# Weight low parts by accumulating DMA in the first mixer, weights prepared 1024 wide, and new beginnings of the stages of a two-layer decoder kernel

## The chip, the cores and the metric

The kernel runs on one core of a Trainium2 chip. The metric is the time of one execution in device microseconds (us). The core has a matmul engine (TensorE, PE in the rows; its weight loads, PEld, overlap the matmuls), VectorE (DVE), ScalarE (ACT), GpSimd (POOL) and SyncE (SP). Each engine works through its own queue of instructions in order. DMA transfers are issued by SP, ACT or POOL and then run beside the engines.

## The reference, cut to what matters

512 tokens of width 1024 pass through two layers in float32. `@` is a matrix product.

```
def even_mixer(h):                        # layer 0
    q, k, v, glu = split(h @ w_in)        # 8 query heads, 2 key/value heads, 64 wide
    a = band_attention(rotary(q), rotary(k), v, window 128, sinks)
    c = glu_a * sigmoid(glu_b)            # 512 channels
    c = causal_depthwise_conv(c, 31 taps) + bias
    return concat(a, silu(layer_norm(c))) @ w_out

def odd_mixer(h):                         # layer 1
    dilated windows (128,1), (512,4), (2048,16) mixed by their softmax sums
    || gMLP: u * (lower-triangular mixing of layer_norm(g) per group)
    concatenated, then @ w_out

def swiglu(h):  return (silu(h @ w_gate) * (h @ w_up)) @ w_down     # 2816 wide

for layer in (0, 1):
    h = h + mixer(rms_norm(h));  h = h + swiglu(rms_norm(h))
y = rms_norm(h)
```

## The kernel before

**Products.** Activations lie transposed, as eight tiles h[0] to h[7] of 128 channels by 512 tokens. Every float32 product is made of three matmuls in the fp32r type: a value is split into a high part (its rounding to fp32r) and a low part (the rest), and high by high, high by low and low by high are summed in one PSUM bank. `acc3` issues the three, at L200 (weight high, activation high), L201 (weight high, activation low) and L202 (weight low, activation high), each 128x128 by 128x512. `norm_tile` splits h[k] after multiplying it with the norm's gain: ACT writes xh (L312), DVE writes xl (L313).

**Weights.** All weights lie in HBM as one stream `ws` of blocks 128x1024, in the order in which they are used. `dma_block` (L161) loads a block into a `raw` buffer from SP's queue. `prep_unit` takes half a block, 512 wide: ACT copies it to the high part (L173) and an engine subtracts that from raw to get the low part (L150). That engine is DVE, but GpSimd in the layer-0 mixer after the first two k steps. Three units are prepared ahead of the one in use, and a unit is 12 matmuls.

**Orders.** The order of PE's instructions is written out by hand; `Seq` places the attention steps, the transposes and the norm between the products by written costs and due times (`C0`, `tick`). The orders of the other engines are set by a scheduler when the kernel is built, from priorities and its own timing of the code. The taps of the convolution have a low priority (`LATER`).

**Start.** The first product goes over k = 0 to 7 into two banks as the tiles of h arrive. The RMS norm's sum of squares is made beside it: DVE and ACT square (L333, L335), GpSimd takes k = 0, 1 and 5, DVE adds the two sums (L340), and four matmuls with a column of ones (L343) give the sum per token. `norm_b` (L355 to L358) makes the row factor R from it, which is applied after the products.

**Layer-0 mixer.** Products of q, k, v and the two convolution inputs, with attention (scores L580 and L581, exponentials L600, transposes L406, values L420) placed between them. The key's low part kl is made by DVE (L688), the query's by L707. `conv_tile` (L470 to L479) makes 31 taps for each of four channel tiles. With `taps=(8, 15, 15, 10)`, that many (the first on ACT alone) go by an ACT product (L473) and a GpSimd add (L474); the rest are multiply-adds of DVE into a PSUM bank (L476, L478).

**FFN.** Two blocks of hidden units (f = 0, 1) go through `acc3`, for gate (pg) and up (pu). The others go in groups by seven products of Strassen's kind (L891 to L894): sums of activations s (S1 and the like) by sums of weights. The operands T1 to T4 of the weights are made in memory: ACT writes rows of h times gain (L799, for the activations), GpSimd issues a DMA that adds one block of `ws` onto another block that lies in a raw buffer (L857), ACT makes the high part (L867), DVE the low part (L150, w2l). `norm_a` and `norm_b` stand behind pg and pu of f = 0, then `act` and `sums` (L826 to L829, L810 to L817) make the activation sums.

Of the kernel before, what the change touches and what calls it, by code (L numbers as in the profile page):

```python
# [10 lines left out]
def _warn_once_fixed(msg, *args, **kwargs):  # L11
# [12 lines left out]
P = 128  # L24
S = 512
# [16 lines left out]
    sq_pool=(0, 1, 5), rope_v=('k', 'q2', 'q3'),  # L42
    taps=(8, 15, 15, 10),

    norm=(6.15, 2.0), q=5.99, v=0.5, S=3.13, ST=0.86, TA=0.65, AO=1.09, LB=4.85, LO=2.1, ln=(54.8, 69.91, 96.75, 112.86),
# [43 lines left out]
def order_ffn_in():  # L89
    o = [(w, k, f) for f in GROUPS[0] for w in range(2) for k in range(KT)]  # L90
    return o + [(w, 4 * kh + j, f) for fs in GROUPS[1:] for w, kh in BLOCKS for j in range(4) for f in fs]
# [42 lines left out]
def trunk_kernel(ctx: ExitStack, tc: tile.TileContext, xT, ws, cols, sinks, sgu_g, sgu_b,  # L134
# [18 lines left out]
    RAW_AHEAD, PREP_AHEAD = 3, 3  # L153
# [11 lines left out]
    def prep_unit():  # L165
        u = st["prep"]
        b, half = divmod(u, 2)
        while st["dma"] <= b:
            dma_block()
        src = raws[b][:, half * 512:half * 512 + 512]  # L170
        hi = wpool.tile([P, 512], F32R, name="w_hi", bufs=PREP_AHEAD + 1)
        lo = wpool.tile([P, 512], F32R, name="w_lo", bufs=PREP_AHEAD + 1)
        A.activation(hi, src, AF.Copy)  # L173
        sub(lo_engine[0], lo, src, hi)
        units[u] = (hi, lo)
        st["prep"] += 1
        if half:
            del raws[b]
            if st["dma"] < len(STREAM) and st["dma"] <= b + RAW_AHEAD:
                dma_block()  # L180

    def next_unit():
        u = st["tile"] // 4
        while st["prep"] < min(2 * len(STREAM), u + PREP_AHEAD + 1):
            prep_unit()
        return units[u]

    def next_tile():
        t = st["tile"]
        hi, lo = next_unit()  # L190
        st["tile"] += 1
        j = t % 4
        if j == 3:
            del units[t // 4]
        return hi[:, j * P:(j + 1) * P], lo[:, j * P:(j + 1) * P]
# [48 lines left out]
    def next_row():  # L244
        hi, lo = next_unit()
        st["tile"] += 4
        del units[st["tile"] // 4 - 1]
        return hi, lo
# [35 lines left out]
    st["dma"] = 1  # L284
    nc.sync.dma_start(raw[:, :512], ws[0, :, :512])
    nc.sync.dma_start(cc, cols)
    nc.sync.dma_start(h[0], xT[0])
    nc.sync.dma_start(raw[:, 512:], ws[0, :, 512:])
    for k in range(1, KT):
        nc.sync.dma_start(h[k], xT[k])  # L290
        if k in (2, 4):
            dma_block()
# [5 lines left out]
    V.memset(mhalf, -0.5)  # L298

# [17 lines left out]
    def norm_sq(k, eng=None):  # L317
        if eng is G:
            first = "accg" not in norm
            if first:  # L320
                norm["accg"] = mpool[0].tile([P, S], F32, name="pts", bufs=3)
                G.tensor_mul(norm["accg"], h[k], h[k])
            else:
                sq = mpool[0].tile([P, S], F32, name="prod", bufs=3)
                G.tensor_mul(sq, h[k], h[k])
                G.tensor_add(norm["accg"], norm["accg"], sq)
            return
# [9 lines left out]
    def norm_a(b):  # L337
        acc = norm.pop("acc")
        if "accg" in norm:
            V.tensor_add(acc, acc, norm.pop("accg"))  # L340
        ms = bank(b)
        for t in range(NQ):
            T.matmul(ms[:, t:t + 1], acc[:, t * P:(t + 1) * P], ones, start=True, stop=True)  # L343
        mse = scr.tile([P, 4], F32, name="mse")
# [98 lines left out]
    with ExitStack() as mx:  # L443
# [15 lines left out]

        yc = [mp.tile([P, S], F32, name=f"yc{j}") for j in range(4)]  # L460
# [40 lines left out]
        def sq_eng(k):  # L501
            return G if k in C0["sq_pool"] else None

# [3 lines left out]
        def norm_line():  # L507
            yield 0.0, C0["norm"][0]
            norm_a(6)
            yield 0.75, C0["norm"][1]  # L510
# [9 lines left out]

        for k in range(KT):
            if k < 3:
                norm_tile(k, "ev_g", sq_eng(k))
            if k == 2:
                for q in range(3, KT):
                    norm_tile(q, "ev_g", sq_eng(q))
                seq.add("N", norm_line())
            for n in C0["first"].split():
                acc3(first[n], xs[k], k == 0, k == KT - 1)
            if k == 1:  # L530
                lo_engine[0] = G
# [31 lines left out]
        def scores0(i):  # L563
# [3 lines left out]
            qss = qTs[i][1]  # L567
# [103 lines left out]
        for step in C0["steps"].split():  # L671
# [24 lines left out]
            elif kind == "q":  # L696
                ps = gemm_in(step)
                seq.until(lambda: len(qTs) < 2)
                qTs[i] = (mp.tile([P, S], F32, name="qT", bufs=3),
                          [mp.tile([P, S], F32R, name=f"qs{b}", bufs=2) for b in range(2)])  # L700

                def after(i=i, ps=ps, step=step):
                    qT, qss = qTs[i]
# [18 lines left out]
            elif kind == "Y":  # L722
# [4 lines left out]
                early[i] = mp.tile([P, S], F32, name="qT", bufs=3)  # L727
# [39 lines left out]
    def ffn(layer, gnext):  # L767
        with ExitStack() as fx:
# [9 lines left out]
            def temps():  # L778
                return {"p1": [scr.tile([P, S], F32, name="ga") for _ in range(2)],
                        "p5": [scr.tile([P, S], F32, name="gb") for _ in range(2)],  # L780
                        "u2": [fp.tile([P, S], F32, name="ta", bufs=2) for _ in range(2)],
                        "g2": [fp.tile([P, S], F32, name="tb", bufs=2) for _ in range(2)]}
# [139 lines left out]

            hidden(0)
            for f in GROUPS[0]:
                pg, pu = bank(2 * f), bank(2 * f + 1)
                for k in range(KT):
                    acc3(pg, xs[k], k == 0, k == KT - 1)
                if f == 0:
                    norm_a(6)
                for k in range(KT):  # L930
                    acc3(pu, xs[k], k == 0, k == KT - 1)
                if f == 0:
                    norm_b(7)
                act(f, pg, pu)
                sums(f)
                if f == 0:
                    prep_ops(2)
# [381 lines left out]
```

## Time and profile before

| | us |
|---|---|
| time before, median of 3 | 1125.21 (1124.75 to 1131.72) |
| the profiled execution's own time | 1123.48 |
| its span, first to last instruction | 1121.8 |
| PE busy | 1073.6 (96%) |
| DVE busy | 701.2 (63%) |
| ACT busy | 571.7 (51%) |
| POOL busy | 244.7 (22%) |

The span is what the trace shows, and the profiled execution lasted 1.68 us longer than its span. The median stands 1.73 us above the profiled execution. The mean granted clock of TensorE was 0.979 of full speed. A busy share counts an engine as busy at either clock; it is an average over stages with different limits.

### The profile page before, as it was taken

The numbers are of one execution on the slowest core, as the hardware profiler recorded it, in microseconds if no ns is written. First come the engines' busy times: TensorE is split into PE (matmuls) and PEld (weight loads), VectorE is DVE, ScalarE is ACT, GpSimd is POOL, SyncE is SP. The second block draws the span as 40 slices with busy tenths as digits, with TensorE's granted clock in tenths as the row PEclk, the third lists the DMA queues.
The fourth block names the chain that finished last, engine by engine and source line by source line (L and its number), as shares of the span: only waits on it lengthen the run. The fifth ranks groups of instructions, "written<-read, shape, count | busy, mean of one in ns | idle before, by whom it ended". The sixth has DMA issues, their size and how long they took to land.

```text
span 1121.8 us, 13570 instructions
## 1 busy us (share of the span) xinstructions
PE 1073.6 (96%) x5052; PEld 888.4 (79%) x5052; DVE 701.2 (63%) x1060; ACT 571.7 (51%) x926; POOL 244.7 (22%) x218
## 2 busy tenths in 40 slices
PE   6988999899999999999999999999899999999997
PEld 4867778788888888888887888887688888888785
DVE  6899866677565655664748647655765556555543
ACT  5577756654434353543637654455544443535433
POOL 4898754201101010100024200002111010101002
PEclk9988899899999999999999999999999999999999
DMA  5221112977857676711532111247778577767121
GB/s 216 81 71 57 38 38 92 246 210 190 182 170 162 184 150 199 145 43 57 164 99 75 39 55 59 79 154 184 216 189 180 165 167 182 154 189 150 25 69 75
DMA packets 42802, 145.87 MB, mean 130 GB/s; under 512 B 4848, under 2 KB 5744, under 8 KB 42736
## 3 DMA queue, kind: packets, MB, share of 16 engines
q1 hardware_dynamic: 31216, 103.06, 27.1%
q0 software_dynamic: 11520, 41.95, 22.2%
q8 instruction: 39, 0.64, 0.2%
q14 instruction: 27, 0.22, 0.1%
HBM read 142.89 MB, written 2.10 MB: 129 GB/s over the span
## 4 chain that ended last, share of the span: by engine, by line
PE 77%; DVE 8%; ACT 4%; issue 4%; POOL 4%; DMA 2%; POOLq 0%; SPq 0%; ACTq 0%; DVEq 0%
PE bank L894 11%; PE bank L891 11%; PE bank L893 11%; PE bank L200 10%; PE bank L201 10%; PE bank L202 10%; PE bank L261 2%; PE bank L263 2%; PE bank L262 2%; PE bank L420 2%; POOL yc L474 1%; DMA raw<-in_ws 1%; PE bank L906 1%; PE bank L406 1%; DVE w2l L150 1%
## 5 line engine op out<-in xcount | busy, mean ns | idle before, releaser
L150 DVE TENSOR_TENSOR w2l<-raw,w2h 128x1024 fp32r<-128x1024 f32 x140 | 171.5, 1226 | 200.6 <-ACT w2h L867 199.8
L867 ACT ACTIVATE w2h<-raw 128x1024 fp32r<-128x1024 f32 x140 | 148.0, 1059 | 204.7 <-PE bank L894 161.7
L173 ACT ACTIVATE w_hi<-raw 128x512 fp32r<-128x512 f32 x204 | 128.1, 629 | 185.3 <-PE bank L201 138.8
L857 POOL DMA_DIRECT2D raw<-in_ws x80 | 70.0, 887 | 558.7 <-DMA raw<-in_ws 270.0
L150 DVE TENSOR_TENSOR w_lo<-raw,w_hi 128x512 fp32r<-128x512 f32 x161 | 115.0, 715 | 61.5 <-ACT w_hi L173 61.5
L891 PE MATMUL bank<-w2h,s 128*128 128x512 f32 x320 | 126.2, 394 | 1.7 <-ACT ga L957 1.5
L893 PE MATMUL bank<-w2l,s 128*128 128x512 f32 x320 | 125.3, 391 | 1.8 <-DVE w2l L150 1.8
L894 PE MATMUL bank<-w2h,s 128*128 128x512 f32 x320 | 125.3, 392 | 0.1
L200 PE MATMUL bank<-xh,w_hi 128*128 128x512 f32 x272 | 113.6, 418 | 10.8 <-ACT xh L312 10.8
L201 PE MATMUL bank<-xl,w_hi 128*128 128x512 f32 x272 | 110.8, 407 | 1.9 <-DVE xl L313 1.9
L202 PE MATMUL bank<-xh,w_lo 128*128 128x512 f32 x272 | 110.2, 405 | 0.0
L200 PE MATMUL bank<-hh,w_hi 128*128 128x512 f32 x256 | 99.8, 390 | 0.0
L202 PE MATMUL bank<-hh,w_lo 128*128 128x512 f32 x256 | 99.6, 389 | 0.0
L201 PE MATMUL bank<-hl,w_hi 128*128 128x512 f32 x256 | 99.6, 389 | 0.0
L891 PE MATMUL bank<-w2h,xh 128*128 128x512 f32 x240 | 94.4, 393 | 0.0
L894 PE MATMUL bank<-w2h,xl 128*128 128x512 f32 x240 | 93.5, 390 | 0.0
L893 PE MATMUL bank<-w2l,xh 128*128 128x512 f32 x240 | 93.4, 389 | 0.0
L891 PEld LDWEIGHTS bank<-w2h,s 128*128 128x128 f32 x320 | 60.4, 189 | 14.9 <-ACT ga L957 1.9
L893 PEld LDWEIGHTS bank<-w2l,s 128*128 128x128 f32 x320 | 60.5, 189 | 14.5 <-DVE w2l L150 2.1
L200 PEld LDWEIGHTS bank<-xh,w_hi 128*128 128x128 f32 x272 | 54.1, 199 | 22.4 <-ACT xh L312 11.7
L894 PEld LDWEIGHTS bank<-w2h,s 128*128 128x128 f32 x320 | 60.5, 189 | 13.1 <-DVE s L150 0.4
L150 POOL TENSOR_TENSOR w_lo<-raw,w_hi 128x512 fp32r<-128x512 f32 x43 | 58.9, 1371 | 43.3 <-ACT w_hi L173 37.8
(234 smaller groups left out, 2069.6 us busy)
## 6 DMA issues: line engine op xcount, KB each, us to landing
raw<-in_ws SPq DMA_DIRECT2D x181, 512.0 KB, 4.0
raw<-in_ws POOLq DMA_DIRECT2D x80, 512.0 KB, 5.4
h<-in_xT SPq DMA_DIRECT2D x8, 256.0 KB, 6.5
out_y<-xh SPq DMA_DIRECT2D x4, 256.0 KB, 2.0
out_y<-xl SPq DMA_DIRECT2D x4, 256.0 KB, 2.3
raw<-in_ws SPq DMA_DIRECT2D x2, 256.0 KB, 4.0
ropeC<-in_rope_c SPq DMA_DIRECT2D x2, 256.0 KB, 4.0
ropeS<-in_rope_s SPq DMA_DIRECT2D x2, 256.0 KB, 4.8
```

Of the source, the lines that this page charges most:

```text
L150: eng.tensor_tensor(out=out, in0=a, in1=b, op=ALU.subtract)
L173: A.activation(hi, src, AF.Copy)
L200: T.matmul(ps, hi, xh, start=start, stop=False)
L201: T.matmul(ps, hi, xl, start=False, stop=False)
L202: T.matmul(ps, lo, xh, start=False, stop=stop)
L261: T.matmul(ps[t], xh[:, c], hi, start=(k == 0), stop=False)
L262: T.matmul(ps[t], xh[:, c], lo, start=False, stop=False)
L857: nc.gpsimd.dma_start(t, ws[base + 8 * (g - 1) + 2 * BLOCK_OF[more] + q], accum_op=ALU.add)
L867: A.activation(hi, src, AF.Copy)
L891: T.matmul(ps[t], xh[:, c], wh[:, w], start=(start and j == 0), stop=False, skip_group_check=True)
L893: T.matmul(ps[t], xh[:, c], wl[:, w], start=False, stop=False, skip_group_check=True)
L894: T.matmul(ps[t], xl[:, c], wh[:, w], start=False, stop=(j == 3), skip_group_check=True)
```

## The change

- **Preparation 1024 wide.** `prep_unit` takes a whole block; two blocks are prepared ahead of the one in use, with two raw buffers and three buffers each of high and low parts. Block 0 is still prepared in halves.
- **Low parts by accumulating DMA.** In the layer-0 mixer, once the first loop over k is over, ACT makes a second copy with scale -1 of the high part (L178 of the new kernel), and GpSimd issues a DMA (L179) that adds the block of `ws` onto it in memory. This is so for 20 blocks. Elsewhere the low part is DVE's subtraction.
- **Taps.** `taps=(12, 18, 18, 14)`: 14 more taps go by ACT product and GpSimd add, 58 of DVE's 72 L478 stay.
- **Start.** Five float32 matmuls of 128x256 on zeros stand ahead of the first product. Loads: cc from ACT's queue, h[0] first on SP's. The squares are all made by ACT, and summed by PE, four matmuls with ones for each k (`sq_sum`), between the products.
- **FFN beginnings.** Of f = 0, gate and up take k = 0 to 6 first and k = 7 last. `norm_a` follows f = 0, and `norm_b` with f = 0's activation and sums stands in the middle of f = 1. The operands of T1 are begun ahead of f = 0. One temporary (g2) is dropped.
- Some tiles are placed in other memory: qT in gb, `early` in prod, Pm and qs earlier, uT0 in the place of mask1.

The diff, cut to what the prediction speaks of:

```diff
...
-    sq_pool=(0, 1, 5), rope_v=('k', 'q2', 'q3'),
-    taps=(8, 15, 15, 10),
+    rope_v=('k', 'q2', 'q3'),
+    taps=(12, 18, 18, 14),
...
     def prep_unit():
...
+        b = st["prep"]
         while st["dma"] <= b:
             dma_block()
...
+        hi = wpool.tile([P, 1024], F32R, name="w_hi", bufs=PREP_AHEAD + 1)
+        lo = wpool.tile([P, 1024], F32R, name="w_lo", bufs=PREP_AHEAD + 1)
+        for c in ((slice(0, 512), slice(512, 1024)) if b == 0 else (slice(0, 1024),)):
+            A.activation(hi[:, c], raw[:, c], AF.Copy)
+            if lo_engine[0] is G:
+                A.activation(lo, hi, AF.Copy, scale=-1.0)
+                nc.gpsimd.dma_start(lo, ws[STREAM[b]], accum_op=ALU.add)
+            else:
+                sub(V, lo[:, c], raw[:, c], hi[:, c])
...
+    idle = scr.tile([P, 256], F32, name="sq", bufs=1)
+    V.memset(idle, 0.0)
+    ps = bank(7)
+    for _ in range(5):
+        T.matmul(ps[:, :256], idle[:, :P], idle, start=True, stop=True)
...
+        def sq_sum(k):
+
+            sq = mp.tile([P, S], F32, name="prod", bufs=3)
+            A.activation(sq, h[k], AF.Square)
+            for t in range(NQ):
+                T.matmul(ms[:, t:t + 1], sq[:, t * P:(t + 1) * P], ones, start=(k == 0 and t == 0),
+                         stop=(k == KT - 1), skip_group_check=True)
...
+            prep_ops(2)
+            for q in range(2):
+                source(1, "T1", q)
             hidden(0)
             for f in GROUPS[0]:
...
+                if f == 0:
+
+                    o = [(w, k) for w in range(2) for k in range(KT - 1)] + [(w, KT - 1) for w in range(2)]
+                else:
+                    o = [(w, k) for w in range(2) for k in range(KT)]
+                for i, (w, k) in enumerate(o):
+                    acc3(ps[w], xs[k], k == 0, k == KT - 1)
+                    if f == 1 and i == KT - 1:
+                        norm_b(7)
+                        act(0, *first)
+                        sums(0)
                 if f == 0:
                     norm_a(6)
...
+            act(1, *ps)
+            sums(1)
...
```

On GpSimd's queue in the layer-0 mixer, where the first taps (of the tile yc_125, in the new kernel yc_134) begin, the kernel before has

```order
L474 TENSOR_TENSOR yc_125<-yc_125,prod 128x512 x2
L150 TENSOR_TENSOR w_lo<-raw,w_hi 128x512
L474 TENSOR_TENSOR yc_125<-yc_125,prod 128x512
L150 TENSOR_TENSOR w_lo<-raw,w_hi 128x512
L391 TENSOR_TENSOR rb<-rb,ropeS 128x512
L474 TENSOR_TENSOR yc_125<-yc_125,prod 128x512
L150 TENSOR_TENSOR w_lo<-raw,w_hi 128x512
L392 TENSOR_TENSOR qT<-ra,rb 128x512
```

and the new kernel

```order
L179 DMA w_lo<-in_ws 128x1024 x2
L483 TENSOR_TENSOR yc_134<-yc_134,prod 128x512 x3
L396 TENSOR_TENSOR rb<-rb,ropeS 128x512
L483 TENSOR_TENSOR yc_134<-yc_134,prod 128x512
L179 DMA w_lo<-in_ws 128x1024
L397 TENSOR_TENSOR gb<-ra,rb 128x512
L483 TENSOR_TENSOR yc_134<-yc_134,prod 128x512
L179 DMA w_lo<-in_ws 128x1024
L483 TENSOR_TENSOR yc_134<-yc_134,prod 128x512 x4
```

The subtractions are gone, and one DMA for 1024 columns stands for two of them; each still waits behind the adds (L483) ahead of it.

On ACT's queue at the same place the kernel before has one copy of a half block at a time between the tap products (L473):

```order
L470 ACTIVATE yc_125<-cp_116,cc 128x512
L473 ACTIVATE prod<-cp_116,cc 128x512 x3
L556 ACTIVATE Vt<-bank_410 128x512
L173 ACTIVATE w_hi<-raw 128x512
L473 ACTIVATE prod<-cp_116,cc 128x512
```

and the new kernel has two instructions of twice the width for a block (tap products are L482):

```order
L479 ACTIVATE yc_134<-cp_122,cc 128x512
L482 ACTIVATE prod<-cp_122,cc 128x512 x4
L176 ACTIVATE w_hi<-raw 128x1024
L482 ACTIVATE prod<-cp_122,cc 128x512
L178 ACTIVATE w_lo<-w_hi 128x1024
L482 ACTIVATE prod<-cp_122,cc 128x512 x2
L176 ACTIVATE w_hi<-raw 128x1024
```

The negated copy (L178) is new, and a tap product can stand between it and the high part.

On PE where FFN 0 begins, the kernel before takes the last tile of h (xh_1869) at the end of the gate's product into bank_1882, ahead of all of the up product:

```order
L202 MATMUL bank_1882<-xh_1844,w_lo 128x512
L200 MATMUL bank_1882<-xh_1869,w_hi 128x512
L201 MATMUL bank_1882<-xl_1870,w_hi 128x512
L202 MATMUL bank_1882<-xh_1869,w_lo 128x512
L343 MATMUL bank_1918<-ones,nacc 128x1 x4
L200 MATMUL bank_1883<-xh_1727,w_hi 128x512
```

The new kernel takes it (xh_1859) for gate and up (bank_1888, bank_1889) once both have had the other seven:

```order
L208 MATMUL bank_1889<-xh_1838,w_lo 128x512
L206 MATMUL bank_1888<-xh_1859,w_hi 128x512
L207 MATMUL bank_1888<-xl_1860,w_hi 128x512
L208 MATMUL bank_1888<-xh_1859,w_lo 128x512
L206 MATMUL bank_1889<-xh_1859,w_hi 128x512
L207 MATMUL bank_1889<-xl_1860,w_hi 128x512
L208 MATMUL bank_1889<-xh_1859,w_lo 128x512
L345 MATMUL bank_1950<-ones,nacc 128x1 x4
L206 MATMUL bank_1959<-xh_1727,w_hi 128x512
```

The last tile of h is wanted 21 matmuls later than before, the sum of squares (L345) 24 later.

## Rows read from the trace of the kernel before

**Rows 1.** Windows by stretch: length; busy us (x instructions) per engine; granted clock; DMA share; GB/s.

```profile
26.40:62.40 36.00, 36.00 (x166) 29.88 (x165) 30.95 (x42) 19.39 (x32) 30.49 (x23) 1.00 0.24 74
62.40:106.00 43.60, 35.57 (x188) 29.41 (x187) 41.04 (x92) 35.21 (x80) 39.30 (x30) 0.92 0.19 61
106.10:112.40 6.30, 6.30 (x32) 6.21 (x30) 6.20 (x8) 3.23 (x6) 5.52 (x4) 0.50 0.27 85
112.90:153.80 40.90, 36.09 (x200) 30.80 (x200) 35.85 (x81) 27.94 (x68) 25.53 (x20) 0.88 0.08 27
195.70:226.60 30.90, 27.49 (x113) 22.09 (x113) 21.81 (x33) 20.10 (x32) 7.26 (x7) 0.89 0.94 250
```

**Rows 2.** PE's waits: line, releaser, us in all, times, longest.

```profile
PE bank L581 <- DVE kl L688: 3.5, 2, 2.2
PE bank L406 <- ACT yn L634: 3.4, 2, 2.4
```

**Rows 3.** Timeline of PE at the start: begin, us, operation, [idle before].

```profile
7.41 0.80 PE L200 MATMUL bank<-xh,w_hi 128*128 128x512 f32 x1 [7.41 <-ACT xh L312]
13.28 0.63 PE L202 MATMUL bank<-xh,w_lo 128*128 128x512 f32 x1
15.17 0.39 PE L200 MATMUL bank<-xh,w_hi 128*128 128x512 f32 x1
15.40 0.40 PE L201 MATMUL bank<-xl,w_hi 128*128 128x512 f32 x1
19.38 0.50 PE L201 MATMUL bank<-xl,w_hi 128*128 128x512 f32 x1 [1.08 <-DVE xl L313]
24.82 1.05 PE L343 MATMUL bank<-ones,nacc 128*128 128x1 f32 x8 [1.67 <-DVE nacc L340]
25.73 0.48 PE L200 MATMUL bank<-xh,w_hi 128*128 128x512 f32 x1
```

**Rows 4.** Groups by line and shape, 26.4 to 153.8 us: busy us, mean ns, idle before.

```profile
L474 POOL TENSOR_TENSOR yc<-yc,prod 128x512 f32<-128x512 f32 x44 | 60.2, 1369 | 7.9 <-ACT prod L473 6.4
L478 DVE SCALAR_TENSOR_TENSOR bank<-cp,cc,bank 128x512 f32<-128x512 f32 x72 | 54.1, 752 | 1.3
L150 POOL TENSOR_TENSOR w_lo<-raw,w_hi 128x512 fp32r<-128x512 f32 x26 | 36.0, 1387 | 9.2 <-ACT w_hi L173 9.2
L173 ACT ACTIVATE w_hi<-raw 128x512 fp32r<-128x512 f32 x26 | 16.3, 625 | 8.8 <-PE bank L201 8.5
L473 ACT ACTIVATE prod<-cp,cc 128x512 f32<-128x512 f32 x44 | 30.6, 714 | 5.1 <-POOL yc L474 4.9
L707 DVE TENSOR_TENSOR qs<-qT,qs 64x512 fp32r<-64x512 f32 x8 | 9.3, 1156 | 0.5 <-ACT qs L706 0.2
```

**Rows 5.** Page, costliest groups: busy us, mean ns, idle before.

```profile
L867 ACT ACTIVATE w2h<-raw 128x1024 fp32r<-128x1024 f32 x140 | 148.0, 1059 | 204.7 <-PE bank L894 161.7
L857 POOL DMA_DIRECT2D raw<-in_ws x80 | 70.0, 887 | 558.7 <-DMA raw<-in_ws 270.0
```

**Rows 6.** Page, DMA issues: KB each, median us to landing.

```profile
raw<-in_ws POOLq DMA_DIRECT2D x80, 512.0 KB, 5.4
```

**Rows 7.** Timelines of PE, ACT and DVE where FFN 0 begins.

```profile
203.50 0.49 PE L200 MATMUL bank<-xh,w_hi 128*128 128x512 f32 x1 [2.78 <-ACT xh L312]
198.45 4.38 ACT L799 ACTIVATE raw<-h,cc 128x512 f32<-128x512 f32 x7
216.56 0.69 DVE L826 TENSOR_TENSOR ga<-bank,R 128x512 f32<-128x512 f32 x1 [0.39 <-ACT R L358]
226.65 0.39 PE L891 MATMUL bank<-w2h,xh 128*128 128x512 f32 x1
228.66 0.68 DVE L150 TENSOR_TENSOR s<-ga,s 128x512 fp32r<-128x512 f32 x1
```

**Rows 8.** Timelines of ACT and PE where FFN 1 begins.

```profile
775.09 1.06 ACT L867 ACTIVATE w2h<-raw 128x1024 fp32r<-128x1024 f32 x1 [5.92 <-DMA raw<-in_ws]
791.22 0.50 PE L893 MATMUL bank<-w2l,s 128*128 128x512 f32 x1 [1.78 <-DVE w2l L150]
```

More of the change, by code (lines that the diff above doesn't have):

```diff
@@ L315, in norm_tile, with norm_sq @@
         norm_sq(k, sq)
[L317 to L326, printed above, removed]
+    def norm_sq(k, sq=None):
+        if sq is False:
             return
@@ L458, in trunk_kernel @@
         V.tensor_scalar(out=taps, in0=taps, scalar1=0.5, scalar2=None, op0=ALU.mult)
+        mp.tile([P, 8, 2 * P], F32, name="Pm", bufs=2)
+        for b in range(2):
+            mp.tile([P, S], F32R, name=f"qs{b}", bufs=2)
         yc = [mp.tile([P, S], F32, name=f"yc{j}") for j in range(4)]
@@ L698, in trunk_kernel @@
                 seq.until(lambda: len(qTs) < 2)
-                qTs[i] = (mp.tile([P, S], F32, name="qT", bufs=3),
-                          [mp.tile([P, S], F32R, name=f"qs{b}", bufs=2) for b in range(2)])
+                qTs[i] = [mp.tile([P, S], F32R, name=f"qs{b}", bufs=2) for b in range(2)]
                 def after(i=i, ps=ps, step=step):
-                    qT, qss = qTs[i]
+                    qT, qss = scr.tile([P, S], F32, name="gb"), qTs[i]
                     rope(ps, qT, tabs, V if step in C0["rope_v"] else G)
@@ L726, in trunk_kernel @@
                     acc3(ps, (oh[k], ol[k]), k == 0, k == 3)
-                early[i] = mp.tile([P, S], F32, name="qT", bufs=3)
+                early[i] = mp.tile([P, S], F32, name="prod", bufs=3)
                 A.activation(early[i], ps, AF.Copy)
@@ L780, in temps @@
                         "p5": [scr.tile([P, S], F32, name="gb") for _ in range(2)],
-                        "u2": [fp.tile([P, S], F32, name="ta", bufs=2) for _ in range(2)],
-                        "g2": [fp.tile([P, S], F32, name="tb", bufs=2) for _ in range(2)]}
+                        "u2": [fp.tile([P, S], F32, name="ta", bufs=2) for _ in range(2)]}
+            homes = [fp.tile([P, 1024], F32R, name=x, bufs=3) for x in ("w2h", "w2l")]
+            del homes
             sop = {}
@@ L1076, in trunk_kernel @@
         Vt = mp.tile([P, NQ, S], F32, name="Vt")
+        mp.tile([P, 10 * P], F32, name="Pm", bufs=3)
         for t in range(NQ):
@@ L1187, in trunk_kernel @@
             V.tensor_add(gt[:, t, :], gt[:, t, :], sbB)
-        uT = [mp.tile([P, S], F32, name=f"uT{j}") for j in range(4)]
+        uT = [mp.tile([P, S], F32, name=f"uT{j}" if j else "mask1") for j in range(4)]
         def mixing():
```

105 lines of the change are left out of this document (43 added, 62 removed).

## The prediction

> **What bounds the kernel now.** I first read the shares of busy time: TensorE 96%, so what can be won is where it waits or runs at half its clock. I looked for those places with windows by stage. In the layer-0 mixer's first products, 26.4 to 62.4, PE is busy for 36.00 of 36.00 us at full clock: nothing to win. From 62.4 to 106.0 it is busy 35.57 of 43.60, from 112.9 to 153.8 36.09 of 40.90; these leave 8.0 and 4.8 us idle. The clock row adds to that: 0.92 and 0.88 mean that a part of the stretch ran at half clock (1.2 of 2.4 GHz), and at half clock half of the time is lost, so the loss is (1 - clock) times the stretch, 3.5 and 4.9 us; the stretch between, 106.1 to 112.4, lies wholly at 0.50 and loses 3.2 [rows 1]. The mixer thus loses 12.8 idle + 11.6 clock = 24.4 us. There DVE is the fullest engine, 41.04 of 43.60 (94%), ACT 35.21, POOL 39.30 [rows 1]. PE's waits name kl from DVE (3.5 us in two) and yn from ACT (3.4) [rows 2]: the waits are for engines that carry the convolution's taps beside attention. The beginnings of stages come next: the start waits 7.41 us for the first tile of h, then runs at half clock (matmul records of 0.63 us until 13.28, 0.39 later), and waits 1.08 for a low part and 1.67 for the squares [rows 3]; FFN 0 waits 2.78 for the last xh and falls to a clock of 0.89 in 30.9 us, 3.4 us lost [rows 7, 1]; FFN 1 has ACT waiting 5.92 for a raw block and PE 1.78 for a low part [rows 8]. The rest, the FFN bodies and layer 1's mixer, is 0 in the sum, +-2 in the range: their instructions change only in width.
>
> **Start: +1 (-1 to +3).** The row of four one-column matmuls (L343) holds PE from 24.82 to 25.73, 0.91 us [rows 3]. There will be eight, so 7 x 0.91 = +6.4 on PE, which is the path here. Off go the waits for the squares and the low part, 1.67 + 1.08 of the rows [rows 3], with some 1.5 of shorter ones (estimate): -4.3, since the tiles of h arrive earlier against PE's work. The clock: the five products on zeros are not in the trace. If they do nothing, half clock still ends some 1 us earlier, since the first product starts a little sooner: -1. Sum +1.1. The nearest row on what float32 work does to the clock is the stretch at 106.1: PE busy all of 6.30 us, with float32 transposes and 64-column products, at a clock of 0.50 [rows 1]. So I take no lift from them; were they to lift it, the 5.9 us from 7.41 to 13.28 would give back half, -2.9.
>
> The Trainium skill ("TensorE: Matmul & The Clock Gate", Part 1: The HAM clock gate) has throttled as the default state, which activity releases; by it the zeros would have the clock up at the first real product, and the start would be -1.9 instead of +1. The trace's busy stretch at 0.50 speaks against that for float32 work of this kind; no row here shows a wide float32 product.
>
> **Low parts in time: +1 (0 to +3).** A block's chain is now: high copy 1.06 (a 1024-wide ACT copy [rows 5]), negated copy 1.06, issue on POOL 0.89 [rows 5], landing 5.4 [rows 6]; the issue is counted besides the landing to be safe. Ahead of each ACT step stands at most a tap product of 0.71, ahead of the issue one add of 1.37 [rows 4]: 8.4 at best, 11 with all in front. It has two blocks' time: 2 x 24 matmuls x 0.23 [rows 3] = 11.0 us. So it mostly just fits; a block or two around the first taps slips by half a microsecond. The landing is the weak number: it is read from transfers that mostly ran alone.
>
> **Layer-0 mixer from 62.4 on: -9 (-17 to +6).** Loads from 26.4 to 153.8 (126.8 us in the rows): DVE 30.95 + 41.04 + 6.20 + 35.85 = 114.0, ACT 85.8, POOL 100.8 [rows 1]. DVE loses 14 taps x 0.752 = 10.5 [rows 4]: 103.5. POOL loses 26 subtractions (36.0), gains 14 x 1.369 = 19.2 and 13 issues x 0.89 = 11.5: 95.5. ACT gains 14 x 0.714 = 10.0 and, for 13 blocks, 2 x 1.059 instead of 2 x 0.625 each, +11.3 [rows 4, 5]: 107.1. The three come out nearly even; the fullest is then ACT at 107 instead of DVE at 114. What falls from the path: kl has 31 - 12 = 19 taps of DVE in channel tile 0 instead of 23 in front, 3.0 us, which takes most of the 3.5 of waits (-2.5; about 1 us stays, since ACT's khh is now the later input). The clock's fall behind this wait, 3.5 in that stretch [rows 1], then has no gap to start it: -3.5. Of the other 9.3 us of idle time (12.8 less kl's 3.5), where PE waits on ACT and DVE by turns, I take a third: -3. Sum -9. The better end: two thirds of the 24.4 go, -17. The worse end: ACT's longer copies stand ahead of the exponentials and yn; 1.06 instead of 0.625 at some 14 places where PE waits for ACT would be 14 x 0.43 = +6.
>
> DVE's two-input instructions are slow here: 64x512 took 1.156 us (L707) against 0.69 for 128x512 in FFN 0 [rows 4, 7]. This is why fewer GpSimd instructions could also help DVE: of 70 adds and subtractions 58 stay.
>
> The Trainium skill ("SBUF — State Buffer", Who interferes with whom) says that a DVE instruction with two SBUF inputs contends with a GpSimd instruction that reads SBUF, and that a DMA stalled by DVE is one whose descriptors GpSimd had to write. The first agrees with 1.156 against 0.69; the second speaks against the change, whose 20 transfers are of this kind, and by it low parts would land late where DVE is full. The 80 like them in the FFNs landed in 5.4 at the median [rows 6], with DVE less full.
>
> **FFN 0's beginning: -5 (-7.25 to -3).** Taking k = 7 last gives 21 matmuls, 4.8 us, of cover to the wait for xh, 2.78 behind seven ACT rows (L799) of 4.38 [rows 7], plus the shorter waits by it (1.1, estimate), and the fall of the clock behind it, 3.4 [rows 1]: up to 7.25. PE then reaches the first product of sums earlier, but the sums come from R: from R's first reader (216.56) to the last sum of S1 (228.66) it is 12.1 us on DVE, and 0.7 for itself [rows 7]. Before, the first products of the groups began at 226.65; 24 of them use xh alone and cover 5.5 us more [rows 7, 3], so S1 was wanted at 232.2, 15.6 after R's first reader, with 2.8 to spare. In the new order norm_b stands 24 matmuls later against these products: 5.5 us less, 10.1 for 12.8. DVE has a low part or so less in between, so I put the new wait at 2.3: -7.25 + 2.3 = -5.
>
> **FFN 1's beginning: -2 (-5 to 0).** T1's operands are issued ahead of f = 0, so the 5.92 that ACT waited for the raw block [rows 8] shrinks; R, queued behind that copy on ACT, comes earlier, and the wait of 1.78 for w2l [rows 8] goes. The transfers of T3 now stand ahead of it in memory traffic, so I take 2.
>
> **Sum.** +1 + 1 - 9 - 5 - 2 = -14: 1123.48 - 14 = 1109.5 for the profiled execution. The median stood 1.73 above that execution, so **1111** for the median. Downwards the terms' ranges, added as squares (2, 1, 8, 2, 3), give 9; upwards the forecast ends where rival A begins. Its own range is 1102 to 1119.
>
> **Rivals.**
> A. *The load only moves from DVE to ACT.* For it: ACT ends at 107 us of work in a stretch that should shrink to 118, 91%, with every tap product and negated copy in one queue with the exponentials, Pm and yn that PE waits for. Against it: tap products have low priority and ACT was at 67%. The mixer then gains nothing; the start, the low parts and the FFN beginnings remain: 1123.48 + 1 + 1 - 5 - 2 + 1.7 = 1120.
> B. *Slower: low parts come too late.* One mechanism, in the layer-0 mixer: GpSimd's queue is in order, and an issue stands behind adds, its landing behind the other transfers. It decides when the chain exceeds 11.0 us. If transfers under a full DVE take 8 us instead of 5.4, the chain is 11 + 2.6 = 13.6, 2.6 late; over the 13 blocks up to 153.8 at half that cost in the mean that is 13 x 1.5 = 20 us, and each gap can take the clock down with it (say 4 x 2): 1111 + 28 = 1139. Against it: the median landing, and POOL's own load falls.
> C. *The clock stays up.* The zeros lift it at the start (-2.9 against my term), and with fewer gaps all of the mixer's 11.6 us of half clock go, 8 more than I took: 1111 - 11 = 1100.
>
> **How the numbers follow.** Forecast 0.50, A 0.27, B 0.09, C 0.14. The bound of 1%, about what a measurement of this kernel can tell from no change, lies at 1113.96 and 1136.5. Faster by over 1%: the part of the forecast's range below 1113.96, 0.36, and C: 0.50. Slower by over 1%: most of B, 0.08. Within 1%: the rest, 0.42. The range goes from below C (1100 less 3 for its own error) to above A (1120 plus 7 for A with a worse start and low parts that slip now and then): 1097 to 1127, leaving out B and the tail of C.
>
> **What would show it.** Right: first product near 7.2, half clock ending by 13; PE's waits for kl under 1.5 us in all and no half clock at 65 to 72; DVE under 85% and ACT about 90% between 62 and 154; landings of the 20 transfers at 5 to 6 us; no wait of PE on w_lo over 1 us; FFN 0's beginning without the 2.78, a wait of about 2 for a sum instead. Wrong: PE waiting on the negated copy's DMA in many places (B), ACT named in most of PE's waits of the mixer with the same idle sum (A), a granted clock of 1.0 from the first real product on (C). The term I trust least is the mixer's -9, for two thirds of it are guesses on which waits follow when the largest goes.

## The result: slower by 1.2%

The changed kernel took 1138.11 us in the median of 4 runs (1135.04 to 1142.93), the kernel before 1125.21. The ratio is 1.0119, with a 95% interval from 1.0093 to 1.0146. I had forecast 1111 and given 0.08 to slower by over 1%.

The profiled execution of the changed kernel lasted 1142.93 us and is the slowest of its four. I set the starts of the same matmul in the two traces against each other. Where the difference jumps, time was lost or won:

| place (start in the trace, us) | before | changed | difference |
|---|---|---|---|
| transposes of v, behind the first products | 34.27 | 36.28 | +2.0 |
| first scores with kl | 65.07 | 65.91 | +0.8 |
| last transposes of the layer-0 mixer | 173.57 | 187.65 | +14.1 |
| first product of FFN 0's groups | 226.65 | 235.54 | +8.9 |
| last product of FFN 0's groups | 513.27 | 532.81 | +19.5 |
| last spatial mixing of layer 1 | 710.31 | 729.53 | +19.2 |
| first product of FFN 1's groups | 780.37 | 796.29 | +15.9 |
| last matmul | 1113.71 | 1131.50 | +17.8 |

The windows by stage of the changed kernel, in the columns of [rows 1]:

```profile
31.40:65.10 33.70, 32.40 (x149) 26.36 (x147) 30.71 (x40) 25.17 (x35) 25.73 (x21) 1.00 0.69 155
65.10:110.00 44.90, 36.88 (x185) 31.24 (x186) 39.17 (x89) 41.02 (x82) 33.48 (x29) 0.89 0.52 114
110.00:166.00 56.00, 48.59 (x236) 42.22 (x235) 37.65 (x81) 36.62 (x81) 32.98 (x27) 0.74 0.24 50
235.50:262.00 26.50, 19.78 (x76) 15.05 (x76) 22.24 (x32) 15.15 (x22) 3.50 (x4) 0.87 0.86 207
```

From 65 to 110 ACT is now the fullest engine, 41.02 of 44.90 us (91%), where it was DVE [rows 1]. PE idles 8.0 and 7.4 us in the two mixer rows. The clock of 0.74 over 56 us costs 14.6 us, against 4.9 + 3.2 in the two rows of before that answer to it [rows 1].

PE's waits in the changed kernel, as in [rows 2]:

```profile
PE bank L906 <- ACT s L825: 7.0, 2, 3.9
PE bank L425 <- ACT pts L414: 4.7, 6, 1.3
PE bank L411 <- ACT yn L648: 4.0, 2, 3.2
PE bank L909 <- DVE s L151: 3.3, 2, 1.7
PE bank L921 <- DVE h L936: 3.3, 8, 0.4
PE bank L411 <- ACT Pm L614: 3.0, 2, 2.8
```

kl (1.1 in all now) has gone from the head of the list, as forecast; ACT stands there instead. One of its waits, in the timelines of ACT and PE:

```profile
73.93 0.71 ACT L482 ACTIVATE prod<-cp,cc 128x512 f32<-128x512 f32 x1
74.54 1.04 ACT L176 ACTIVATE w_hi<-raw 128x1024 fp32r<-128x1024 f32 x1
75.49 1.26 ACT L719 ACTIVATE qs<-gb 64x512 fp32r<-64x512 f32 x2
76.78 0.51 ACT L614 ACTIVATE Pm<-Pm,nm 128x256 f32<-128x256 f32 x1
77.28 1.04 ACT L178 ACTIVATE w_lo<-w_hi 128x1024 fp32r<-128x1024 f32 x1
77.43 0.44 PE L411 MATMUL bank<-ident,Pm 128*128 128x128 f32 x2 [2.84 <-ACT Pm L614]
```

A tap product, a wide copy and the query's parts run between two exponentials; PE waits 2.84 us for the next one, and the granted clock is 0.50 from 79.9 to 86.7. Two more waits of PE in this mixer:

```profile
108.05 1.97 PE L411 MATMUL bank<-ident,Pm 128*128 128x128 f32 x8 [3.18 <-ACT yn L648]
149.15 0.51 PE L207 MATMUL bank<-ol,w_hi 128*128 128x512 f32 x1 [2.29 <-DVE ol L368]
```

FFN 0's beginning, timelines of POOL, ACT and PE:

```profile
220.04 2.65 POOL L872 DMA_DIRECT2D raw<-in_ws  x3 [0.39 <-DMA raw<-in_ws]
232.87 1.06 ACT L882 ACTIVATE w2h<-raw 128x1024 fp32r<-128x1024 f32 x1 [9.05 <-DMA raw<-in_ws]
233.83 1.04 ACT L176 ACTIVATE w_hi<-raw 128x1024 fp32r<-128x1024 f32 x1
234.78 0.58 ACT L363 ACTIVATE R<-bank 128x512 f32<-128x512 f32 x1
247.72 0.79 PE L906 MATMUL bank<-w2h,s 128*128 128x512 f32 x1 [3.86 <-ACT s L825]
250.60 0.79 PE L909 MATMUL bank<-w2h,s 128*128 128x512 f32 x1 [1.66 <-DVE s L151]
```

R's transposes were over by 230.2 (begun at 229.17, 1.05 long). R was made at 234.78, behind a high copy that had ACT waiting 9.05 us for an accumulating DMA. PE then waits 3.86 and 1.66 for sums, and the clock is at half from 247.2 to 254.0.

### The profile page after: what moved, and what is told of

Read it like the earlier page. It is cut to its first block, busy times and chain, and to the rows that moved or that the text cites. A ratio compares the mean times of both kernels' runs of the same rounds, so it can differ in the third digit from the quotient of the medians.

```text
span 1141.2 us, 13502 instructions
## 1 busy us (share of the span) xinstructions
PE 1087.0 (95%) x5118; PEld 900.5 (79%) x5118; DVE 674.8 (59%) x964; ACT 580.8 (51%) x863; POOL 217.5 (19%) x204
## 4 chain that ended last, share of the span: by engine, by line
PE 76%; DVE 8%; ACT 6%; DMA 5%; issue 4%; POOL 1%; SPq 0%; POOLq 0%; ACTq 0%
PE bank L206 10%; PE bank L207 10%; PE bank L906 10%; PE bank L208 10%; PE bank L909 10%; PE bank L908 10%; DMA raw<-in_ws 5%; PE bank L425 3%; PE bank L266 2%; PE bank L268 2%; PE bank L267 2%; DVE bank L487 1%; PE bank L921 1%; ACT w2h L882 1%; DVE w2l L151 1%
## 5 line engine op out<-in xcount | busy, mean ns | idle before, releaser
L176 ACT ACTIVATE w_hi<-raw 128x1024 fp32r<-128x1024 f32 (+1 forms) x103 | 107.9, 1048 | 131.0 <-PE bank L207 97.5
L151 DVE TENSOR_TENSOR w_lo<-raw,w_hi 128x1024 fp32r<-128x1024 f32 (+1 forms) x83 | 103.8, 1251 | 41.5 <-ACT w_hi L176 37.7
L206 PE MATMUL bank<-xh,w_hi 128*128 128x512 f32 x272 | 111.3, 409 | 1.6 <-ACT w_hi L176 1.6
L207 PE MATMUL bank<-xl,w_hi 128*128 128x512 f32 x272 | 108.0, 397 | 0.0
L483 POOL TENSOR_TENSOR yc<-yc,prod 128x512 f32<-128x512 f32 x58 | 79.0, 1363 | 19.1 <-ACT prod L482 12.5
L208 PEld LDWEIGHTS bank<-xh,w_lo 128*128 128x128 f32 x272 | 52.2, 192 | 13.5 <-DMA w_lo<-in_ws 1.5
```

The source lines that it names most:

```text
L151: eng.tensor_tensor(out=out, in0=a, in1=b, op=ALU.subtract)
L176: A.activation(hi[:, c], raw[:, c], AF.Copy)
L206: T.matmul(ps, hi, xh, start=start, stop=False)
L207: T.matmul(ps, hi, xl, start=False, stop=False)
L208: T.matmul(ps, lo, xh, start=False, stop=stop)
L483: G.tensor_add(yc[j], yc[j], p)
```

## The experiments

Each was timed beside the kernel before on the same chip; the ratio is against that. "Changed" is 1138.1.

| kernel | median us | ratio (95%) |
|---|---|---|
| changed, old taps | 1133.6 | 1.0078 (1.0052 to 1.0104) |
| changed, old taps, subtraction on GpSimd | 1132.4 | 1.0057 (1.0039 to 1.0076) |
| the same, copies in halves | 1134.0 | 1.0077 (1.0050 to 1.0104) |
| the same, sums earlier (copies wide) | 1127.1 | 1.0008 (0.9987 to 1.0029) |
| changed, T1's copy behind R | 1153.4 | 1.0245 (1.0223 to 1.0267) |
| changed, old FFN beginnings | 1143.9 | 1.0167 (1.0133 to 1.0201) |
| 512 wide, old taps, subtraction | 1121.3 | 0.9966 (0.9952 to 0.9981) |
| 512, old FFN beginnings (start alone) | 1125.0 | 1.0007 (0.9989 to 1.0024) |
| 512, no zeros | 1122.2 | 0.9977 (0.9963 to 0.9990) |
| 512, eight zeros | 1120.3 | 0.9959 (0.9943 to 0.9975) |
| 512, eight zeros, sums earlier | 1119.4 | 0.9941 (0.9922 to 0.9960) |
| 512, low parts by DMA, old taps | 1130.2 | 1.0050 (1.0031 to 1.0070) |
| 512, low parts by DMA, new taps | 1132.2 | 1.0057 (1.0038 to 1.0076) |
| 512, second copy without DMA | 1126.7 | 1.0010 (0.9995 to 1.0026) |
| 512, low parts by DMA, four ahead | 1126.9 | 1.0007 (0.9990 to 1.0024) |

**Old taps.**

```diff
-    taps=(12, 18, 18, 14),
+    taps=(8, 15, 15, 10),
```

> The changed kernel with the taps of the kernel before (8, 15, 15, 10 to GpSimd). Theory 1, ACT's queue: in the layer-0 mixer PE waits because ACT got some 21 us of work (14 tap products, 10; wider copies, 11) between exponentials and yn, and the clock falls behind these waits. Half of that work goes: 5 to 7 us faster than the changed kernel, about 1132, with the waits for Pm and yn shorter. But DVE gets 14 taps back, so the wait for kl (1.1 in all) should come back to about 3. Theory 2, late low parts: GpSimd loses 19 us of adds, which helps its issues, but the mixer's loss stays with the transfers: within 2 us of the changed kernel.

4.5 us faster than changed, near the number of theory 1, though the two intervals overlap. Its trace has 1.5 us of waits for Pm instead of 3.0, yn's still 3.6, and kl's back at 2.6. Its mixer ends 5.6 us earlier, but two other executions of the changed mixer (below) end it 7.0 and 4.3 earlier, so this trace doesn't tell the taps from the execution. More taps on ACT and GpSimd do not pay here, though they take 10 us from DVE.

**Old taps and subtraction.** (The transfers are gone; halves are used for GpSimd's subtraction.)

```diff
-                A.activation(lo, hi, AF.Copy, scale=-1.0)
-                nc.gpsimd.dma_start(lo, ws[STREAM[b]], accum_op=ALU.add)
+                for d in (slice(0, 512), slice(512, 1024)):
+                    sub(G, lo[:, d], raw[:, d], hi[:, d])
```

> The changed kernel with the old taps and, in the layer-0 mixer, low parts by GpSimd's subtraction (two of 512 for a block) instead of negated copy and accumulating DMA. What stays of the change is the width of 1024, the start and the FFN beginnings. Theory 1 (ACT's queue): all of the mixer's 12 us go, about 1126, and 5 to 7 more than with the old taps alone. Theory 2 (late low parts): all of the 12 us go here and none with the old taps alone. A third, the width and the shifted order: the loss stays, 1136 or more.

Only 1.2 us more, no difference that can be told: neither theory 1 nor 2 carries most of the loss. The third comes nearest, though not to its 1136: 7.5 of the 13 us against before stay with the width, the start and the FFN beginnings. The trace shows one place, ACT's timeline in FFN 0:

```profile
218.30 1.06 ACT L882 ACTIVATE w2h<-raw 128x1024 fp32r<-128x1024 f32 x1 [4.73 <-DMA raw<-in_ws]
224.09 1.06 ACT L176 ACTIVATE w_hi<-raw 128x1024 fp32r<-128x1024 f32 x1 [4.73 <-PE bank L208]
225.05 0.58 ACT L363 ACTIVATE R<-bank 128x512 f32<-128x512 f32 x1
```

Ahead of R the wide high copy waits 4.73 us until PE has freed a buffer, which with blocks of 1024 happens once in 24 matmuls.

**T1's copy behind R.** (u = 2 is the first block of T1.)

```diff
+                if u == 2:
+                    tie = scr.tile([P, 1], F32, name="mse1", bufs=1)
+                    V.tensor_scalar(out=tie, in0=norm["R"][:, 0:1], scalar1=0.0, scalar2=1.0,
+                                    op0=ALU.mult, op1=ALU.add)
+                    A.activation(hi, src, AF.Copy, scale=tie)
```

> The changed kernel with the third high copy of FFN weights (first block of T1) tied behind R on ACT in both FFNs, by a scale of one that is worked out from R. Theory: R waited some 5 us behind this copy, which waited 9 us for an accumulating DMA; R comes 3 to 5 us earlier in FFN 0, the wait of 3.9 for a sum there shrinks to 1 or less and the half clock behind it goes: 6 to 9 us faster in FFN 0, 2 to 4 in FFN 1, about 1128. Rival: the sums are bound by DVE's work and not by R: less than 2 us.

15 us slower: the edit did not bring R forward. In the trace ACT waits as long, 9.35 us ahead of R, now with a high copy of the first products' weights that waits for its own raw block; PE then waits 6.4 us for a sum, and T1's copies come late. Whichever copy stands first waits for memory: four accumulating transfers and two plain ones were under way together, and those issued last took 12.4 us (GpSimd's) and 11.0 (SP's) from issue to landing, against 5.7 for the first. This does not account for the 15 us: from the mixer's end on, this trace loses 14 against the changed kernel's, 1.4 of them where FFN 0 begins and 2.5 where FFN 1 begins; the rest is spread thin and not explained.

**Old FFN beginnings.** The loop over f and `order_ffn_in` are those of the kernel before.

```diff
-            prep_ops(2)
-            for q in range(2):
-                source(1, "T1", q)
...
-                        norm_b(7)
-                        act(0, *first)
-                        sums(0)
...
```

> The changed kernel with the FFN beginnings of the kernel before, in both FFNs. By the traces FFN 0's beginning costs 5.4 more than before and FFN 1's gains 1.4: about 4 us faster than the changed kernel, 1134. If the new wait for the sums is not of the order but of what stands in the queues (blocks 1024 wide), it stays, and the old waits come back: 3 us slower than the changed kernel, 1141.

5.8 us slower than changed, as the second reading had it: the new beginnings help, even at 1024 wide. What costs in FFN 0 is something else, that hits the old order too (there PE waits 4.7 for the squares' sum and 3.1 for rc).

**512 wide again.** `prep_unit`, `next_unit`, `next_tile` and `next_row` are those of the kernel before.

```diff
-    RAW_AHEAD, PREP_AHEAD = 2, 2
+    RAW_AHEAD, PREP_AHEAD = 3, 3
...
-        hi = wpool.tile([P, 1024], F32R, name="w_hi", bufs=PREP_AHEAD + 1)
+        hi = wpool.tile([P, 512], F32R, name="w_hi", bufs=PREP_AHEAD + 1)
```

> The changed kernel with old taps, low parts by GpSimd's subtraction, and the weights prepared 512 wide, three units ahead, as before. Of the change stay the start and the FFN beginnings (and the placement of some tiles). Theory W, the width: high copies of 1024 wait up to 24 matmuls for a buffer in ACT's queue, ahead of R (4.7 us in FFN 0 with old taps and subtraction), so FFN 0's beginning gives back what it wins. Then FFN 0 is 4 us or more faster than with 1024 wide and the whole about 1124, against 1132.4 with 1024 wide. Rival, memory traffic: the copies wait for the accumulating transfers of T1 whatever the width: within 2 us of 1132.

11.1 us faster than at 1024, and faster than the kernel before. The width is the largest single loss of the change. Between the two traces, 6 of 8 us are won where FFN 0 begins. The third raw buffer comes back with this edit and was not tried apart; in the 1024-wide trace a copy to w_hi waits for its raw block only once, 5.69 us at 571, not where FFN 0 begins.

**Start alone.** 

> As the one before, with the FFN beginnings of the kernel before: only the start (and the placement of tiles) is new. By the traces the start is 2 us behind the kernel before at 35 us and the mixer then follows the same order: 1127. If the start's shift lets the clock fall for longer in the mixer, as in the changed kernel, 1130 or more. Against the kernel with the new FFN beginnings it tells what those are worth at 512 wide: +4 to +9 by theory W, within 2 by memory traffic.

1125.0, as before: the start neither wins nor loses. The FFN beginnings are worth 3.7 at 512 wide.

**Zeros**, none or eight (`range(8)`) instead of five.

```diff
-    for _ in range(5):
+    for _ in range(0):
```

> As the first of these, without the five products on zeros. If the zeros release the clock (the changed kernel's trace has full clock from 4.83 to 8.24, ahead of and into the first real products), without them the first products run at half clock from 7.0 to 13 or so, 1.5 to 2 us slower at 30 us. Rival: float32 zeros do nothing and the phase of the clock alone decides: within 0.5 us at 30 us.

> As the first of these, with eight products on zeros instead of five: PE is busy with them until about 7 us, where it was idle from 5.5 to 7.0. If the half clock from 8.24 to 11.65 followed from that idle time, it goes: first products at full clock throughout, 1.7 us faster at 30 us; the first real product may start up to 0.7 later. Rival: the clock falls all the same, or the zeros delay the first product by more than they save: no gain at 30 us.

Without zeros the first products start at 7.03, with five at 7.02, and the two traces stay together until 70 us: five do nothing in these executions. Eight keep PE busy until the first product, and the clock is full from 5.76 on. PE's timeline with eight:

```profile
5.75 1.47 PE L306 MATMUL bank<-sq 128*128 128x256 f32 x6
7.03 0.50 PE L201 MATMUL bank<-xh,w_hi 128*128 128x512 f32 x1
...
8.09 0.39 PE L201 MATMUL bank<-xh,w_hi 128*128 128x512 f32 x1
8.32 0.40 PE L202 MATMUL bank<-xl,w_hi 128*128 128x512 f32 x1
```

The product's record of 0.39 at 8.09 would be 0.63 at half clock [rows 3]. It is 1.55 us ahead at 25 us, as expected; the median is 1.0 lower, within what it can tell. One trace each says little here: of the 13 traces with five zeros, six have the transposes of v as early as eight have them (0.2 to 0.3 us behind the kernel before, the other seven 1.6 to 2.0), and full clock from before the first product on without a fall. Both traces with eight are early, the one with none is late.

**Low parts by DMA at 512 wide**, with new and with old taps (the transfer is `ws[STREAM[b], :, half * 512:half * 512 + 512]`).

> The changed kernel with the weights prepared 512 wide again, three units ahead; negated copy and accumulating DMA now for half blocks (40 transfers of 256 KB), taps 12, 18, 18, 14. All of the change but the width. If the parts add up (width 11, taps 4.5, low parts 1.2, by the medians so far), 1127. If low parts and taps only hurt because of the width (long copies in ACT's queue, long chains), 1117 to 1121. If half-size transfers cost GpSimd twice the issues and land no faster, low parts come late: 1132 or more, with PE waiting on transfers of w_lo.

> As the one before with the taps 8, 15, 15, 10. Low parts by DMA alone at 512 wide: against the kernel with the subtraction (1121.3) it has 36 us less on GpSimd and 16 us more on ACT. By additivity 1122.5; if GpSimd's subtractions held up DVE at the shared work, faster: 1116 to 1119, with kl and qs on DVE under 1 us each.

8.9 slower than the subtraction with old taps, which no forecast had; 10.9 with new taps, where the third reading (1132 or more) came. The low parts do cost, but the costs do not add: at 1024 wide, where the width has already lost the time, they cost 1.2. PE's waits with old taps:

```profile
PE bank L425 <- ACT pts L414: 7.0, 5, 4.0
PE bank L207 <- DMA w_lo<-in_ws: 4.7, 4, 2.1
```

PE waits four times for a transfer, and waits for pts on ACT grew from 2.5 in all (subtraction) to 7.0.

**Sums earlier**, at 512 (with eight zeros) and at 1024 wide.

```diff
                         act(0, *first)
-                        sums(0)
                 if f == 0:
                     norm_a(6)
+                    sums(0)
                     first = ps
+            sums(1)
             act(1, *ps)
-            sums(1)
```

> The best so far (512 wide, old taps, subtraction, eight products on zeros: 1120.3) with the activation sums S made ahead of R's readers, since they need h alone: for f = 0 behind the norm's sum, for f = 1 ahead of its activation. If the waits at the first products of sums come from the order of DVE and ACT (sums queued behind R and its readers), they go: waits of 0.6 + 2.1 and half the half-clock stretch in FFN 0 (1.7), 2.4 + 1.9 + 3.4 in FFN 1: 4 to 9 us faster, about 1114. Rival, traffic: T1's blocks land no earlier, PE waits for w2h or w2l in place of s: 1118 or more.

> 1024 wide, old taps, subtraction (1132.4) with the same earlier sums. In that kernel a high copy waited 4.7 us for a free buffer ahead of R, and PE 5.1 for a sum. If the width's 11 us are mostly this, they go when the sums don't hang on R: 1123 to 1126. If they come from the width elsewhere (the mixers, the clock), no more than in the 512-wide pair: 1127 or more.

At 512 0.8 us, no difference that can be told: traffic was right. The waits for sums are gone and those for T1's parts stand in their place:

```profile
PE bank L904 <- DVE w2l L151: 6.7, 4, 3.2
...
PE bank L902 <- ACT w2h L878: 2.1, 2, 1.2
```

At 1024 it wins 5.4 (1127.1, just beyond the first reading), so about half of the width's 11 hung on sums behind R. This 512-wide kernel, at 0.9941 (0.9922 to 0.9960), is the fastest of the study.

**What the low parts and the width cost it by.** Three more, on the second copy, the landing and the length of the copies:

```diff
-        sub(lo_engine[0], lo, src, hi)
+            A.activation(neg, hi, AF.Copy, scale=-1.0)
+            G.tensor_add(lo, src, neg)
...
-    RAW_AHEAD, PREP_AHEAD = 3, 3
+    RAW_AHEAD, PREP_AHEAD = 3, 4
...
-        for c in ((slice(0, 512), slice(512, 1024)) if b == 0 else (slice(0, 1024),)):
+        for c in (slice(0, 512), slice(512, 1024)):
```

> 512 wide, old taps, start and FFN beginnings new, as the kernel that took 1121.3; low parts by GpSimd again, but as raw plus a negated copy that ACT makes: the second copy of the change without its transfers. Theory C, the copy on ACT costs: 1127 to 1131, as with the transfers. Theory L, the landing costs: within 2 us of 1121.

> 512 wide, old taps, negated copy and accumulating DMA (1130.2), with four units ahead instead of three (one more buffer of each part), so 12 more matmuls, 2.7 us, for the landing. Theory L: PE's waits for w_lo, 4.7 us in all, go under 1, and the time falls by 4 to 8. Theory C: the waits for w_lo go, but the time stays within 2 us of 1130.

> 1024 wide buffers, old taps, subtraction (1132.4), but every block is copied and subtracted in two halves of 512. If it is the long instructions of the width (1.06 instead of 0.62 on ACT, 1.23 instead of 0.69 on DVE ahead of others in the queues), 1122 to 1125. If it is the coarser release (a buffer comes free every 24 matmuls, and the copy that waits for it holds up ACT's queue), 1130 or more.

The second copy alone costs 5.4 of the 8.9 us, though GpSimd works as before; one more unit ahead wins back 3.4, and PE no longer has a wait for w_lo over 1 us. Copies in halves win nothing at 1024 wide (1134.0). By the medians each of theories C and L has a part, 5.4 and 3.4, both just short of what they forecast, and the length of the copies is out. The traces put much of the loss elsewhere. The table sets them against the kernel before, in the first table's places: the mixer from the transposes of v to its last transposes, FFN 0 from there to the last product of its groups. Four accumulating transfers stand where FFN 0 begins; the third is T1's first block, whose high copy stands ahead of R on ACT:

| kernel (one trace each) | mixer | FFN 0 | third transfer issued behind the first | lands after | ACT waits for it |
|---|---|---|---|---|---|
| 512, old taps, subtraction | +2.1 | -1.6 | 5.4 | 5.7 | 4.76 |
| 512, second copy without DMA | +1.8 | +4.9 | 2.0 | 11.9 | 10.48 |
| 512, low parts by DMA, old taps | +8.7 | +0.9 | 2.1 | 10.2 | 4.37 |
| 512, low parts by DMA, four ahead | +1.3 | +3.9 | 1.8 | 12.4 | 11.17 |
| changed, old taps, subtraction | +2.5 | +5.3 | 5.0 | 6.0 | 4.73 |
| the same, copies in halves | +1.3 | +6.0 | 3.9 | 9.5 | 8.03 |
| changed | +12.1 | +5.5 | 1.8 | 12.3 | 9.05 |

Two of these waits, in the timelines of ACT (512 with subtraction, and with the second copy):

```profile
216.77 1.06 ACT L878 ACTIVATE w2h<-raw 128x1024 fp32r<-128x1024 f32 x1 [4.76 <-DMA raw<-in_ws]
```

```profile
220.91 1.06 ACT L883 ACTIVATE w2h<-raw 128x1024 fp32r<-128x1024 f32 x1 [10.48 <-DMA raw<-in_ws]
```

In the 512-wide mixer the traces point to the landing: 8.7 with the transfers, 1.3 with a fourth unit ahead and the same copies on ACT, 1.8 with the copies alone, 2.1 with neither. What the second copy loses, and the kernel with four ahead too, is lost in FFN 0, after the last negated copy. Against the subtraction's trace the second copy loses 3.7 us there by a wait of 1.83 for the squares' sum and the half clock behind it, and 2 at the first sums; with four ahead these are 1.0 and 4.5. At the sums R is late: the four transfers are issued closer together in both, T1's first block lands later although it is issued sooner, and R waits behind it. Why they come closer together was not tested, and four ahead was not tried with the subtraction. So theory C's number nearly came, but its mechanism is not shown.

The run with halves doesn't single out the release of buffers either. Ahead of R no copy waits for a buffer in it; T1's transfer (8.03) takes the place of that wait (4.73, above, behind 4.73 for the transfer). In both 1024-wide traces R comes about 6 us behind its transposes (6.4 and 5.8), against 1.3 at 512. Which of the two waits the width brings about stays open. More buffers of that width, the direct test, were not tried.

## Why the prediction was wrong

By terms, in the trace: start +1, came +2.0; mixer and low parts -8, came +12.1; FFN 0 -5, came +5.5; FFN 1 -2, came -1.4; the rest 0, came -0.3. The mixer's term and FFN 0's failed.

- **The step that failed in FFN 0: the width had no term at the beginnings of stages.** "Their instructions change only in width", 0, was said of the FFN bodies and layer 1's mixer, and there it held within its +-2. But I checked the width only as the chain of one low part and as longer copies in the layer-0 mixer, and gave it no term anywhere else. It costs 11.1 us with the subtraction (1132.4 against 1121.3) and 3.4 to 5.9 with the low parts by DMA. About half of the 11.1 (5.4) goes once the sums no longer hang behind R, and by the traces it sits largely in FFN 0 (+5.3 against -1.6). There ACT's in-order queue stands still ahead of R, until PE frees a wide buffer (4.73, old taps and subtraction) or T1's transfer lands (8.03 with halves, 9.05 in the changed kernel). The rest was not located.
- **Layer-0 mixer, forecast -9, in the trace +12** (from +2.0 at 34 us to +14.1). The part on kl was right: waits of 1.1 instead of 3.5, and the half clock at 65 to 72 is gone; PE stood 2.2 us ahead of before at 71. Then the waits moved to ACT (2.84 for Pm, 3.18 for yn; 2.3 for ol came from DVE), with half clock from 79.9, 107.2 and 155.0. The step that failed is reading the fullest engine's load (107 of 118) as room: in the in-order queue a copy or a tap stands straight ahead of four of the 16 exponentials between 65 and 110, and a copy ahead of that yn. My worse end, +6, had the sign. Its mechanism, longer copies on ACT, is seen in these waits but not shown to be the whole: with old taps the mixer loses 6.5 with the low parts by DMA and 2.5 with the subtraction, and at 512 wide the copies alone lose nothing there, and the landing seems to. Size varies: the executions of old FFN beginnings and of T1's copy tied have the changed mixer too, and end it 7.0 and 4.3 us earlier than this one, matmul by matmul, 1.8 and 1.7 of that from the start; so the mixer's loss is 6.9 to 12.1. Half clock at 155 to 168.7 here lasts 3.4 us in those two.
- **GpSimd's adds and DVE.** I counted 58 instead of 70 operations and hoped for faster DVE. qs took 1.302 us in the changed kernel, against 1.156 [rows 4]: fewer GpSimd operations did not help it; why was not tested. By the Trainium skill's rule on two-input instructions ("SBUF — State Buffer", Who interferes with whom) every one of the 58 adds can hold it up, which agrees with 1.302 against 0.69 alone [rows 7]. The count does not decide how far: the same 58 adds stand beside 0.987 at 512 wide with new taps.
- **Low parts in time, +1.** In the changed kernel PE waited once for a transfer, 1.1 us; the median landing was 5.8. So rival B, whose 1139 lies next to the measured 1138, was not what happened there: its mechanism shows only at 512 wide, as 4.7 us of waits and most of the mixer's 8.7. Its number was right by accident, and its sum takes 1.5 for half of 2.6; with 1.3 it gives 1136. Rival A, by PE's waits, was nearest, with a loss where it had none.
- **FFN 0, forecast -5.** The first part came: from the mixer's end (+14.1) to the first group product (+8.9) PE won 5.2, with the second half of the mixer's products in between. The new wait I put at 2.3 was 3.9 + 1.7, with 3.4 of clock and 1.6 more behind it, 10.6 by the table. I had taken DVE's chain behind R as the limit. That chain, from R's first reader (236.24) to the last sum of S1 (250.54), took 14.3 us instead of 12.8. But R itself came 4.6 us behind its transposes, for I had taken no wait ahead of it on ACT, so S1 was wanted 7.6 us behind R's first reader instead of 10.1. As a whole the FFN beginnings are worth -3.7 at 512 and -5.8 at 1024, against my -7 for both.
- **FFN 1, forecast -2:** -1.4 (19.2 to 17.8). **Start, forecast +1:** +2.0 at 34 us (0.2 to 0.3 in six other traces), nothing in the median. Both in their ranges.
- **The zeros:** I took no lift from float32 products, by a stretch of transposes at 0.50 [rows 1]. That was the wrong neighbour: in the trace with eight wide products of zeros the clock is full at 5.76, before any other product.

One step at a time, by medians: before 1124.9, start 1125.0, FFN beginnings 1121.3, width 1132.4, low parts 1133.6, taps 1138.1. In another order (low parts 1130.2, taps 1132.2, then width 1138.1) the shares differ: what costs first takes the time that the next would have taken.

## What to carry to other kernels

Ask of every copy in an in-order queue what it waits for, a buffer that PE must free or a transfer, and what stands behind it; here a wider unit of work cost 11.1 us with less busy time on ACT (554 us in its trace against 573). Moving work from the fullest engine to one at 67% moves the waits with it when the second one feeds the critical chain. Price such parts together: here the width alone loses 11.1 and the low parts alone 8.9 of the 12.3 that both lose. And look at the place as well as the median: two runs whose medians came near a theory's number lost their time in a stage of which it says nothing.

## What was not expected of the hardware

- Float32 matmuls of 128x256 on zeros raise TensorE's clock (full from 5.76 us on with eight of them), while 6.3 us of float32 transposes and 64-column products without a pause ran at 0.50 [rows 1]. With five, and idle time behind them, the changed kernel's clock was full from 4.83 to 8.24 and fell again until 11.65; in six other traces with five it stayed full. The Trainium skill ("TensorE: Matmul & The Clock Gate", Part 1: The HAM clock gate) has the throttled state as the default that activity releases; the eight zeros agree.
- A transfer issued sooner can land later. T1's first block, 512 KB, landed after 5.7 us when it was issued 5.4 us behind the first of its group, and after 11.9 when it was issued 2.0 us behind it; it then landed 4.1 us later in all (220.9 against 216.8).
- Half the size does not halve an accumulating transfer. The DMA issues of the changed kernel and of the 512-wide one with low parts by DMA:

```profile
w_lo<-in_ws POOLq DMA_DIRECT2D x20, 512.0 KB, 5.8
```

```profile
w_lo<-in_ws POOLq DMA_DIRECT2D x40, 256.0 KB, 5.0
```
